# Gate and up projections of a two-layer encoder by seven half-size products for eight

## Chip, cores and metric

One NeuronCore of a Trainium2 chip runs the whole program. The metric is device time in microseconds, the median of several executions; lower is better.

## The reference

The program computes two post-norm layers over 512 tokens of width 1024. Each layer mixes tokens (three groups of attention heads and an output projection), adds the result to the scaled input, normalises, and then applies a SwiGLU feed-forward of width 2816. Weights, inputs and outputs are float32. What the change touches is the first half of the feed-forward:

```python
x = layer_norm(DN_ALPHA * x + mix, ln1_g[l], ln1_b[l])
ff = (jax.nn.silu(x @ ffn_w_gate[l]) * (x @ ffn_w_up[l])) @ ffn_w_down[l]
x = layer_norm(DN_ALPHA * x + ff, ln2_g[l], ln2_b[l])
```

## The kernel before

A float32 operand is split into two float32r parts, a rounded high part (a cast by ACT) and the residual (a subtraction), and a product is three matmuls into one PSUM bank: high by high, high by residual, residual by high (`mm3`, L162). Weights come by the SP queue as raw float32 tiles of 128x1024 (four of them in turn); `wload` (L142) casts them into `whi` on ACT and takes the residual `wlo` on DVE or POOL. The pools `wh` and `wl` hold four tiles of each kind; some loads put both parts into the pool `pqk` instead (ring "q").

The transposed input of the feed-forward, `xT`, lies as high and residual part, each for all 512 tokens. The 22 blocks of 128 hidden columns are done in two parts, 12 and 10. For each block, `gate_up` (L770) runs 8 slices of depth by 3 matmuls of 512 tokens for gate and the same for up, 48 matmuls; `swiglu` (L776) applies SiLU on ACT (L778), multiplies on DVE (L779), and splits the product into the two parts of an `act` tile on ACT and DVE (L781, L782). Blocks 0 and 1 of a layer run by halves of the tokens, 96 matmuls of 256 columns each, so that they can start before the last tokens are normalised. After each part `down` (L800) multiplies its `act` tiles by rows of the down weights, two row blocks per load; the casts go to the rings `DR` in turn.

POOL does norms, residuals of weights and softmax scaling in the attention stage; in the gate/up blocks it has nothing. The program is written as one stream; a scheduler in the tile framework reorders it once per engine, and each engine then runs its own list in order, with semaphore waits. A tile of a pool can be written again when the last reader of the tile that held its place has finished.

The lines that the text names: L156 is the residual of a weight tile (`lo.tensor_tensor` in `wload`), L152 its cast; L214, L215, L217 and L218 are gain and offset of a layer norm on POOL and DVE; L256 is the softmax scaling on POOL; L272 the residual of transposed probabilities on DVE, from PSUM; L290 a sum from PSUM and SBUF on DVE.

Of the kernel before, what the change touches and what calls it, by code (L numbers as in the profile page):

```python
# [10 lines left out]
F32 = mybir.dt.float32  # L11
# [5 lines left out]
P = 128  # L17
# [64 lines left out]
def encoder(ctx: ExitStack, tc, x, w_in, mla_q_norm, mla_kv_norm, w_uq, w_ukv, gqa_q_norm, gqa_k_norm, rel_bias,  # L82
# [5 lines left out]
    def pool(name, bufs, **k):  # L88
        return ctx.enter_context(tc.tile_pool(name=name, bufs=bufs, **k))
# [72 lines left out]
    def mm3(ps, a, b, first, last):  # L162
        ah, al = a
        bh, bl = b
        TE.matmul(ps, ah, bh, start=first, stop=False)  # L165
        TE.matmul(ps, ah, bl, start=False, stop=False)  # L166
        TE.matmul(ps, al, bh, start=False, stop=last)  # L167

    def make_xT():
        return [pxt.tile([P, NT, KD, P], F32R, tag="x", name=n) for n in ("xTh", "xTl")]  # L170

    def put_xT(xT, t):
        for g in range(2):
            pb = bank(ps_pt, "xtr")
            for f in range(4):
                c = (g * 4 + f) * P
                TE.transpose(pb[:, f * P:(f + 1) * P], xt[:, t, c:c + P], ident)
            pb = pb.rearrange("p (f c) -> p f c", f=4)
            h = xT[0][:, t, g * 4:g * 4 + 4, :]
            A.copy(h, pb)  # L180
            V.tensor_tensor(xT[1][:, t, g * 4:g * 4 + 4, :], pb, h.bitcast(F32), op=ALU.subtract)

    def xst(xT, k, t):
        return xT[0][:, t, k, :], xT[1][:, t, k, :]

# [207 lines left out]
    for l in range(DEPTH):  # L393
# [128 lines left out]

        def mla_T(h):
            assert ("q", h // 3) in told
            to_T(lambda t: tq[0][:, t, h, :], 96, mqk[h])
# [46 lines left out]
            V.tensor_tensor(v, v, tm, op=ALU.add)  # L572

        def latent_qv():
            q = pxt.tile([P, NT, 6, 96], F32, tag="x", name="tq")
            tq.append(q)
            wq = [wload(krows(w_uq[l], 0, 2, 288 * c, 288 * c + 288), (P, 2, 288), LO['uq']) for c in range(2)]
            wkv.append(wload(krows(w_ukv[l], 0, 1, 0, 768), (P, 1, 768), LO['kv']))
            yield
            for c in range(2):  # L580
                h, o = wq[c]
                for t in range(NT):
                    pb = bank(ps_mm, "uq")[:, :288]
# [153 lines left out]
        def finish(t):  # L737
            for half in range(2):
                assert ("op", t, half) in told
                cs = slice(half * 512, half * 512 + 512)  # L740
                V.tensor_tensor(xt[:, t, cs], xt[:, t, cs], accs[t][half], op=ALU.add)
            layer_norm(t, gb)
            if not xT2:
                xT2.append(make_xT())
            put_xT(xT2[0], t)

        def out_early():
            out_rest(0, (0, 1))
# [11 lines left out]
        for t in (2, 3):  # L760
            out_rest(t, (0, 1, 2))
            finish(t)
        xT = xT2[0]


        f0 = 0
        for part, nf in enumerate((12, 10)):
            act = []

            def gate_up(w, pss, tsl):  # L770
                for wt, ps in zip(w, pss):
                    for k in range(KD):
                        xm = (xT[0][:, tsl, k, :], xT[1][:, tsl, k, :])
                        mm3(ps[:, tsl.start * P:tsl.stop * P], (wt[0][:, k], wt[1][:, k]), xm, k == 0, k == KD - 1)

            def swiglu(pss):  # L776
                sg = ppl.tile([P, T], F32, tag="l", name="sg")
                A.activation(sg, pss[0], AF.Silu)  # L778
                V.tensor_tensor(sg, sg, pss[1], op=ALU.mult)  # L779
                a = pmix.tile([P, 2, T], F32R, tag="m", name="act")  # L780
                A.copy(a[:, 0], sg)  # L781
                V.tensor_tensor(a[:, 1], sg, a[:, 0].bitcast(F32), op=ALU.subtract)  # L782
                act.append(a)

            fs = list(range(f0, f0 + nf))
            if part == 0:
                first = [(w, (bank(ps_sc, "gate"), bank(ps_pv, "up"))) for w in first]
                for tsl in (slice(0, 2), slice(2, 4)):
                    for w, pss in first:
                        gate_up(w, pss, tsl)  # L790
                for w, pss in first:
                    swiglu(pss)
                fs = fs[2:]
            for f in fs:
                w = load_gu(f, V, RINGS[f % 2])
                pss = (bank(ps_sc, "gate"), bank(ps_pt, "up"))
                gate_up(w, pss, slice(0, 4))
                swiglu(pss)

            def down(acc, toks, half, lo, lead=0):  # L800

                n = nf // 2
                ws = {}
                for i in range(n + lead * (len(toks) - 1)):
                    if i < n:
                        ws[i] = wload(krows(w_down[l], f0 + 2 * i, 2, half * 512, half * 512 + 512), (P, 2, 512), lo, DR[i % 5], "wd")
                    for q, (t, pb) in enumerate(zip(toks, acc)):
                        c = i - lead * q
                        if not 0 <= c < n:
                            continue  # L810
                        ts = slice(t * P, (t + 1) * P)
                        for j in range(2):
# [52 lines left out]
```

## Time and profile before

| quantity | value |
|---|---|
| median of 3 runs | 1281.17 us (1280.31 to 1282.43) |
| the profiled execution | 1282.31 us |
| its span, first to last instruction | 1280.5 us |
| PE busy | 1250.1 us, 98%, 6352 matmuls |
| DVE busy | 687.7 us, 54% |
| ACT busy | 543.6 us, 42% |
| POOL busy | 324.6 us, 25% |
| mean granted clock of PE | 0.994 |

Busy time is the time in which an engine has an instruction in flight. Matmuls overlap in the pipeline, so that a matmul's length (0.39 us for 512 columns) is longer than the distance to the next; distances are read from the timeline. PEld is the loading of the stationary operand, which overlaps PE. In the timelines a row is one instruction, or several of the same kind in a row (x2, x4) with their joint time.

### The profile page before, as it was taken

The page shows a single profiled execution, that of the slowest core. Times are in us where ns is not written, and L with a number is a line of the kernel's source. Part 1 is how long each engine was busy: PE and PEld are TensorE (multiplying, and loading weights), DVE is VectorE, ACT ScalarE, POOL GpSimd, SP SyncE. Part 2 cuts the span into 40 slices and gives each one's busy share as a digit, 9 for nine tenths or more (in the row PEclk, how much of TensorE's full clock was granted, in tenths as well). Part 3 has the DMA queues.
Part 4 walks back from the last instruction along what each step waited for, and adds up shares of the span by engine and source line. Part 5 has one row for each costly group of instructions (what it writes and reads, how often), then busy time and mean ns, then how long its engine had stood idle before and what let it go on. Part 6 is the DMA issues. An engine that isn't in the chain of part 4 may idle for free.

```text
span 1280.5 us, 16743 instructions
## 1 busy us (share of the span) xinstructions
PE 1250.1 (98%) x6352; PEld 1062.5 (83%) x6352; DVE 687.7 (54%) x1138; ACT 543.6 (42%) x955; POOL 324.6 (25%) x344
## 2 busy tenths in 40 slices
PE   8999899999999999999999998999999999999997
PEld 7888788889888888888898897888988888888885
DVE  4377997684333333332664889966843332333346
ACT  4465786544222212222245668855342221222222
POOL 0445475661000000000245456655500000000004
PEclk9999899999999999999999999999999999999999
DMA  5623210324333233332425231114243333333223
GB/s 179 188 67 87 87 34 13 120 69 130 99 99 97 89 96 98 99 99 99 148 78 147 84 103 48 28 30 134 77 115 99 99 99 99 99 99 98 92 96 110
DMA packets 140552, 122.57 MB, mean 96 GB/s; under 512 B 6924, under 2 KB 114572, under 8 KB 140472
## 3 DMA queue, kind: packets, MB, share of 16 engines
q1 hardware_dynamic: 140460, 121.48, 32.0%
q8 instruction: 50, 0.82, 0.3%
q14 instruction: 30, 0.25, 0.1%
q10 hardware_dynamic: 12, 0.02, 0.0%
HBM read 114.65 MB, written 2.12 MB: 91 GB/s over the span
## 4 chain that ended last, share of the span: by engine, by line
PE 80%; DVE 8%; DMA 4%; ACT 3%; POOL 2%; issue 2%; SPq 0%; DVEq 0%; POOLq 0%; ACTq 0%
PE gate L165 6%; PE down L167 6%; PE down L166 6%; PE up L167 6%; PE down L165 6%; PE up L165 6%; PE up L166 6%; PE gate L167 6%; PE gate L166 6%; PE sc L241 4%; PE ptr L264 3%; PE po L283 2%; PE po L282 2%; PE tp L166 1%; PE tp L165 1%
## 5 line engine op out<-in xcount | busy, mean ns | idle before, releaser
L152 ACT CAST whi<-wraw 128x1024 fp32r<-128x1024 f32 (+3 forms) x202 | 205.6, 1020 | 550.6 <-PE gate L166 149.3
L156 DVE TENSOR_TENSOR wlo<-wraw,whi 128x1024 fp32r<-128x1024 f32 (+3 forms) x170 | 208.2, 1226 | 319.7 <-ACT whi L152 315.7
L191 POOL TENSOR_TENSOR rstd<-mv,eps_l 128x1 f32<-128x1 f32 x16 | 5.7, 357 | 680.8 <-DVE mv L200 680.8
L256 POOL TENSOR_TENSOR pl<-pl,srec 128x512 f32<-128x512 f32 x128 | 135.7, 1061 | 153.0 <-DVE srec L255 139.2
L166 PE MATMUL gate<-xTl,whi 128*128 128x512 f32 (+1 forms) x384 | 142.8, 372 | 0.0
L166 PE MATMUL up<-xTl,whi 128*128 128x512 f32 (+1 forms) x384 | 142.7, 372 | 0.0
L167 PE MATMUL gate<-xTh,wlo 128*128 128x512 f32 (+1 forms) x384 | 142.7, 372 | 0.0
L167 PE MATMUL up<-xTh,wlo 128*128 128x512 f32 (+1 forms) x384 | 142.7, 372 | 0.0
L165 PE MATMUL up<-xTh,whi 128*128 128x512 f32 (+1 forms) x384 | 142.6, 372 | 0.0
L165 PE MATMUL gate<-xTh,whi 128*128 128x512 f32 (+1 forms) x384 | 142.4, 371 | 0.0
L167 PE MATMUL down<-whi,act 128*128 128x512 f32 x352 | 136.7, 389 | 0.0
L166 PE MATMUL down<-wlo,act 128*128 128x512 f32 x352 | 136.7, 389 | 0.0
L165 PE MATMUL down<-whi,act 128*128 128x512 f32 x352 | 136.7, 389 | 0.0
L779 DVE TENSOR_TENSOR sg<-sg,up 128x512 f32<-128x512 f32 x44 | 30.3, 688 | 136.1 <-PE up L167 134.8
L156 POOL TENSOR_TENSOR wlo<-wraw,whi 128x512 fp32r<-128x512 f32 (+2 forms) x64 | 79.4, 1265 | 78.7 <-ACT whi L152 78.4
L272 DVE TENSOR_TENSOR PTl<-ptr,PTh 128x512 fp32r<-128x512 f32 x128 | 87.2, 682 | 8.7 <-ACT PTh L271 7.6
L271 ACT CAST PTh<-ptr 128x512 fp32r<-128x512 f32 x128 | 74.9, 586 | 38.9 <-PE ptr L264 38.4
L167 PEld LDWEIGHTS up<-xTh,wlo 128*128 128x128 f32 x384 | 72.4, 189 | 12.6
L165 PEld LDWEIGHTS gate<-xTh,whi 128*128 128x128 f32 x384 | 72.3, 188 | 12.5
L166 PEld LDWEIGHTS up<-xTl,whi 128*128 128x128 f32 x384 | 72.3, 188 | 12.5
L166 PEld LDWEIGHTS gate<-xTl,whi 128*128 128x128 f32 x384 | 72.4, 188 | 12.4
L165 PEld LDWEIGHTS up<-xTh,whi 128*128 128x128 f32 x384 | 72.3, 188 | 12.4
(174 smaller groups left out, 2493.6 us busy)
## 6 DMA issues: line engine op xcount, KB each, us to landing
wraw<-in_ffn_w_down SPq DMA_DIRECT2D x54, 512.0 KB, 3.6
wraw<-in_ffn_w_up SPq DMA_DIRECT2D x44, 512.0 KB, 3.9
wraw<-in_ffn_w_gate SPq DMA_DIRECT2D x44, 512.0 KB, 3.9
wraw<-in_w_in SPq DMA_DIRECT2D x20, 512.0 KB, 4.7
wraw<-in_w_out SPq DMA_DIRECT2D x14, 512.0 KB, 3.7
dt<-tdr SPq DMA_DIRECT2D x12, 448.0 KB, 3.9
wraw<-in_w_in SPq DMA_DIRECT2D x8, 416.0 KB, 3.4
wraw<-in_w_in SPq DMA_DIRECT2D x8, 384.0 KB, 3.9
```

Of the source, the lines that this page charges most:

```text
L152: A.copy(h[:, :n], r[:, :n])
L156: lo.tensor_tensor(o[:, c:c + step], r[:, c:c + step], h[:, c:c + step].bitcast(F32), op=ALU.subtract)
L165: TE.matmul(ps, ah, bh, start=first, stop=False)
L166: TE.matmul(ps, ah, bl, start=False, stop=False)
L167: TE.matmul(ps, al, bh, start=False, stop=last)
L241: TE.matmul(sc, a, b, start=i == 0, stop=i == len(ops) - 1)
L256: G.tensor_tensor(pl, pl, r.to_broadcast([P, T]), op=ALU.mult)
L264: TE.transpose(pb[:, kt * P:(kt + 1) * P], pl[:, kt * P:(kt + 1) * P], ident)
L271: A.copy(ph[:, :, c:c + P], pb)
L272: V.tensor_tensor(plo[:, :, c:c + P], pb, ph[:, :, c:c + P].bitcast(F32), op=ALU.subtract)
L282: TE.matmul(po[:, h0:h0 + 256], self.vst(kt), ph[:, kt], start=kt == 0, stop=False)
L779: V.tensor_tensor(sg, sg, pss[1], op=ALU.mult)
```

## The change

Blocks 3 to 21 of each layer are computed by a scheme of seven products. The stacked matrix of gate and up columns (2 x 128) over two halves of the depth (2 x 512) is multiplied with the input in two halves of depth and two halves of tokens (256). Instead of eight products of 128 columns by 512 depth by 256 tokens there are seven, of which three have sums of weight quarters as one operand (S1, S2, S3) and sums of input quarters as the other (tf1, tf2, tf3), one has the weight sum S4, and one the input sum tf4:

- `load_forms` takes the two raw tiles of a block, forms the four sums `ws` of 128x512 on POOL (S1, S3, S2, S4 in this order) and casts seven operands into four pairs of `whi`/`wlo` tiles: one cast of 1024 columns (gate, "11" and "12"), five of 512 ("22", "S1", "S2", "S3", "S4"), and their residuals on DVE.
- `by_blocks` runs the seven `product`s, 12 matmuls of 256 columns each, into four banks u0 to u3. Three of the banks take a second product on top of the first, after the first has been copied out. Three copies on ACT (e1, e2), four sums on DVE with one operand in PSUM and one sum on POOL give gate (`sg`) and up; SiLU, product and split follow as before.
- The input lies as four tiles `xF` by depth half and token half; their sums tf1 to tf4 are made once per layer (`diff`, `split4`), three of them on DVE, tf3's difference on POOL.
- Blocks 0, 1 and now 2 run with the plain scheme by halves of the tokens. The parts have 11 and 11 blocks. Since `act` tiles take the place of `pqk`, the weights of `down` are cast into `wh` and `wl` alone. `tq` and the transposed input of the attention stage are cut into smaller tiles of the same pool, with the same operations.

```diff
-    pxt = pool("pxt", 2)
+    pxt = pool("pxt", 4)
...
-        for part, nf in enumerate((12, 10)):
+        for part, nf in enumerate((11, 11)):
...
+            def load_forms(f):
...
+                g1, g2, u1, u2 = g[:, :512], g[:, 512:], u[:, :512], u[:, 512:]
+                s1, s2, s3, s4 = (pv_sb.tile([P, 512], F32, tag="v", name="ws") for _ in range(4))
+                G.tensor_tensor(s1, u1, u2, op=ALU.add)
+                G.tensor_tensor(s3, g1, u1, op=ALU.subtract)
+                G.tensor_tensor(s2, s1, g1, op=ALU.subtract)
+                G.tensor_tensor(s4, g2, s2, op=ALU.subtract)
+                out = {}
+                for group in ((("11", "12"), g), (("22", "S1"), (u2, s1)), (("S2", "S3"), (s2, s3)), (("S4",), (s4,))):
+                    names, src = group
+                    h = wh.tile([P, 1024], F32R, tag="w", name="whi")
+                    o = wl.tile([P, 1024], F32R, tag="w", name="wlo")
+                    if not isinstance(src, tuple):
+                        A.copy(h, src)
+                        V.tensor_tensor(o, src, h.bitcast(F32), op=ALU.subtract)
+                    for i, n in enumerate(names):
+                        c = slice(512 * i, 512 * i + 512)
+                        if isinstance(src, tuple):
+                            A.copy(h[:, c], src[i])
+                            V.tensor_tensor(o[:, c], src[i], h[:, c].bitcast(F32), op=ALU.subtract)
+                        out[n] = (h[:, c], o[:, c])
+                return out
+
+            def product(ps, w, x, more=False):
+                for k in range(4):
+                    c = slice(k * P, k * P + P)
+                    mm3(ps, (w[0][:, c], w[1][:, c]), (x[0][:, k], x[1][:, k]), k == 0 and not more, k == 3, more)
+
+            def by_blocks(w):
...
+                product(r0, w["11"], xb["11"])
+                A.copy(e1[:, :H], r0)
+                product(r1, w["12"], xb["21"])
+                V.tensor_tensor(g[:, :H], r1, e1[:, :H], op=ALU.add)
+                product(r3, w["S1"], tf[1])
+                product(r2, w["S3"], tf[3])
+                A.copy(e1[:, H:], r2)
+                V.tensor_tensor(e2[:, H:], r3, e1[:, H:], op=ALU.add)
+                product(r0, w["S2"], tf[2], True)
+                A.copy(e2[:, :H], r0)
+                G.tensor_tensor(u[:, H:], e2[:, :H], e2[:, H:], op=ALU.add)
+                product(r2, w["22"], tf[4], True)
+                V.tensor_tensor(u[:, :H], r2, e2[:, :H], op=ALU.add)
+                product(r3, w["S4"], xb["22"], True)
+                V.tensor_tensor(g[:, H:], r3, e2[:, :H], op=ALU.add)
+                A.activation(g, g, AF.Silu)
+                V.tensor_tensor(u, g, u, op=ALU.mult)
+                put_act(u)
...
             for f in fs:
-                w = load_gu(f, V, RINGS[f % 2])
-                pss = (bank(ps_sc, "gate"), bank(ps_pt, "up"))
-                gate_up(w, pss, slice(0, 4))
-                swiglu(pss)
+                by_blocks(load_forms(f))
...
-                        ws[i] = wload(krows(w_down[l], f0 + 2 * i, 2, half * 512, half * 512 + 512), (P, 2, 512), lo, DR[i % 5], "wd")
+                        nk = min(2, nf - 2 * i)
+                        ws[i] = wload(krows(w_down[l], f0 + 2 * i, nk, half * 512, half * 512 + 512), (P, nk, 512), lo, "w", "wd")
```

The scheduled orders below show one block in the middle of the first part, where all repeat from block to block. In a row stand the line, the operation, the tile written, the tiles read, the shape and the engines waited for; numbers tell tiles apart.

DVE before, in one gate/up block and the start of the next (`wlo` residual of a weight tile, `sg` product of SiLU and up, `act` its residual):

```order
L782 TENSOR_TENSOR act_3807<-sg_3804,act_3807 128x512 [waits Activation_49]
L156 TENSOR_TENSOR wlo_4086<-wraw_4082,whi_4084 128x1024 [waits DMAHW0_49,PE_49,Activation_49]
L779 TENSOR_TENSOR sg_3872<-sg_3872,up_3823 128x512 [waits PE_49,Activation_49]
L156 TENSOR_TENSOR wlo_3956<-wraw_3952,whi_3954 128x1024 [waits DMAHW1_49,Activation_49]
L782 TENSOR_TENSOR act_3875<-sg_3872,act_3875 128x512 [waits Activation_49]
```

A block has two residuals, the product and its split there, all four at 512 or 1024 columns.

DVE in the changed kernel, in one block (L861 and L866 residuals of operand forms, L886, L890, L895 and L897 sums with a PSUM bank, L899 the product, L829 its residual):

```order
L890 TENSOR_TENSOR e2_4136<-u3_4134,e1_4135 128x256 [waits Activation_49]
L866 TENSOR_TENSOR wlo_4253<-wraw_4238,whi_4252 128x512 [waits DMAHW5_49,PE_49,Activation_49]
L866 TENSOR_TENSOR wlo_4253<-ws_4240,whi_4252 128x512 [waits Activation_49]
L895 TENSOR_TENSOR up_4138<-u2_4133,e2_4136 128x256 [waits PE_49,Activation_49]
L866 TENSOR_TENSOR wlo_4259<-ws_4241,whi_4258 128x512 [waits Activation_49]
L866 TENSOR_TENSOR wlo_4259<-ws_4242,whi_4258 128x512 [waits Activation_49]
L897 TENSOR_TENSOR sg_4137<-u3_4134,e2_4136 128x256 [waits PE_49]
L866 TENSOR_TENSOR wlo_4265<-ws_4243,whi_4264 128x512 [waits Activation_49]
L886 TENSOR_TENSOR sg_4274<-u1_4269,e1_4272 128x256 [waits PE_49,Activation_49]
L899 TENSOR_TENSOR up_4138<-sg_4137,up_4138 128x512 [waits Activation_49,Pool_49]
L861 TENSOR_TENSOR wlo_4386<-wraw_4373,whi_4385 128x1024 [waits DMAHW6_49,Activation_49]
L829 TENSOR_TENSOR act_4233<-up_4138,act_4233 128x512 [waits Activation_49]
```

Four instructions per block have become twelve. The residuals of the block ahead (`wlo_4253` to `wlo_4265`) and of the block after it (`wlo_4386`) stand between the sums of the block that is being multiplied.

POOL in the changed kernel, at the same place (L893 the half-size sum of up; `ws` the operand sums of a block two ahead); before, POOL had no instruction in this stretch:

```order
L893 TENSOR_TENSOR up_4001<-e2_3999 128x256 [waits DVE_49,Activation_49]
L850 TENSOR_TENSOR ws_4240<-wraw_4238 128x512 [waits DMAHW5_49,DVE_49]
L851 TENSOR_TENSOR ws_4242<-wraw_4236,wraw_4238 128x512 [waits DMAHW4_49,DVE_49,Pool_49]
L852 TENSOR_TENSOR ws_4241<-ws_4240,wraw_4236 128x512 [waits DVE_49,Pool_49]
L853 TENSOR_TENSOR ws_4243<-wraw_4236,ws_4241 128x512 [waits DVE_49,Pool_49]
L893 TENSOR_TENSOR up_4138<-e2_4136 128x256 [waits DVE_49,Activation_49]
```

Each operand sum waits for DVE, which frees its `ws` tile by the residual of the block before.

PE in the changed kernel, between two blocks (`u0_3994` is the bank of the block that ends, `u0_4131` and `u1_4132` are those of the next, `whi_4111` and `wlo_4112` its first pair of parts):

```order
L165 MATMUL u0_3994<-tf_3351,whi_3984 128x256
L166 MATMUL u0_3994<-tf_3350,wlo_3985 128x256
L164 MATMUL u0_4131<-xF_3164,whi_4111 128x256 [waits Activation_49]
L165 MATMUL u0_4131<-xF_3164,whi_4111 128x256
L164 MATMUL u1_4132<-xF_3166,whi_4111 128x256
L165 MATMUL u1_4132<-xF_3166,whi_4111 128x256
L166 MATMUL u0_4131<-xF_3164,wlo_4112 128x256 [waits DVE_49]
L164 MATMUL u0_4131<-xF_3164,whi_4111 128x256
```

The first four matmuls of the next block, which read only high parts, are put ahead; the fifth waits for the residual on DVE. Behind it on PE stand products 22 and S4 of the block that ends.

## Rows read from the trace of the kernel before

**Rows 1.** The page: busy time, share and instructions of each engine.
```profile
PE 1250.1 (98%) x6352; PEld 1062.5 (83%) x6352; DVE 687.7 (54%) x1138; ACT 543.6 (42%) x955; POOL 324.6 (25%) x344
```

**Rows 2.** The page: shares of the chain that ended last, by engine.
```profile
PE 80%; DVE 8%; DMA 4%; ACT 3%; POOL 2%; issue 2%; SPq 0%; DVEq 0%; POOLq 0%; ACTq 0%
```

**Rows 3.** Window: PE, PEld, DVE, ACT, POOL busy us (count), clock, DMA share, GB/s.
```profile
306.40:415.00 108.60, 108.60 (x487) 90.17 (x486) 39.01 (x43) 32.39 (x42) 0.00 (x0) 1.00 0.35 104
```

**Rows 4.** Timeline of DVE there: start us, us, engine, line, operation, tiles [idle before].
```profile
395.04 0.69 DVE L779 TENSOR_TENSOR sg<-sg,up 128x512 f32<-128x512 f32 x1 [3.38 <-PE up L167]
396.47 1.22 DVE L156 TENSOR_TENSOR wlo<-wraw,whi 128x1024 fp32r<-128x1024 f32 x1 [0.74 <-ACT whi L152]
397.61 0.68 DVE L782 TENSOR_TENSOR act<-sg,act 128x512 fp32r<-128x512 f32 x1
405.92 0.69 DVE L779 TENSOR_TENSOR sg<-sg,up 128x512 f32<-128x512 f32 x1 [3.42 <-PE up L167]
```

**Rows 5.** Timeline of ACT there.
```profile
395.39 1.05 ACT L152 CAST whi<-wraw 128x1024 fp32r<-128x1024 f32 x1 [4.49 <-DMA wraw<-in_ffn_w_down]
396.34 0.62 ACT L781 CAST act<-sg 128x512 fp32r<-128x512 f32 x1
```

**Rows 6.** Timeline of PE there, 14 spacings of 512 columns.
```profile
399.76 0.39 PE L166 MATMUL gate<-xTl,whi 128*128 128x512 f32 x1
...
402.93 0.39 PE L165 MATMUL up<-xTh,whi 128*128 128x512 f32 x1
```

**Rows 7.** Timeline of PE, 19 spacings of 256 columns, first gate/up group.
```profile
283.10 0.28 PE L165 MATMUL gate<-xTh,whi 128*128 128x256 f32 x1
...
285.37 0.28 PE L167 MATMUL up<-xTh,wlo 128*128 128x256 f32 x1
```

**Rows 8.** Timeline of DVE while its queue is full.
```profile
253.85 1.23 DVE L156 TENSOR_TENSOR wlo<-wraw,whi 128x1024 fp32r<-128x1024 f32 x1 [0.44 <-ACT whi L152]
254.99 0.41 DVE L290 TENSOR_TENSOR mf<-po,pvt 64x256 f32<-64x256 f32 x1
255.33 0.67 DVE L251 TENSOR_REDUCE nm<-sc 128x1 f32<-128x512 f32 x1
255.93 0.67 DVE L272 TENSOR_TENSOR PTl<-ptr,PTh 128x512 fp32r<-128x512 f32 x1
```

**Rows 9.** Timeline of POOL, four sums back to back.
```profile
44.23 5.05 POOL L156 TENSOR_TENSOR wlo<-wraw,whi 128x512 fp32r<-128x512 f32 x4 [43.32 <-ACT whi L152]
```

**Rows 10.** Three source lines: engine, operation, count, ns min/median/max, first and last start.
```profile
L272 DVE TENSOR_TENSOR PTl<-ptr,PTh x128: 668/681/694, 65.1 to 894.3; 128x512 fp32r<-128x512 f32 x128
L156 DVE TENSOR_TENSOR wlo<-wraw,whi x170: 741/1225/2115, 6.8 to 1258.7; 128x1024 fp32r<-128x1024 f32 x152, 128x832 fp32r<-128x832 f32 x8, 128x768 fp32r<-128x768 f32 x6, 128x576 fp32r<-128x576 f32 x4
L256 POOL TENSOR_TENSOR pl<-pl,srec x128: 1032/1042/2094, 58.7 to 890.5; 128x512 f32<-128x512 f32 x128
```

**Rows 11.** Timeline of DVE: L217 with nothing on POOL.
```profile
281.54 0.73 DVE L217 SCALAR_TENSOR_TENSOR xtok<-xtok,mv,lngb 128x512 f32<-128x512 f32 x1
```

**Rows 12.** Timeline of DVE and POOL: L217 beside a POOL sum.
```profile
635.42 1.79 DVE L217 SCALAR_TENSOR_TENSOR xtok<-xtok,mv,lngb 128x512 f32<-128x512 f32 x1
635.38 1.29 POOL L214 TENSOR_TENSOR xtok<-xtok,lngb 128x512 f32<-128x512 f32 x1
```

**Rows 13.** Timeline of POOL beside the first instruction of group 8.
```profile
252.88 3.09 POOL L256 TENSOR_TENSOR pl<-pl,srec 128x512 f32<-128x512 f32 x2
```

**Rows 14.** Windows around two idle stretches of PE: busy time, clock.
```profile
120.00:127.00 7.00, 4.70 (x27) 3.81 (x25) 2.25 (x10) 1.44 (x8) 1.89 (x3) 1.00 0.31 85
145.50:147.00 1.50, 1.50 (x7) 1.50 (x7) 1.50 (x5) 0.15 (x1) 0.23 (x1) 0.50 0.63 236
```

**Rows 15.** Timeline of PE: end of the first idle stretch, and after the second.
```profile
125.87 0.66 PE L264 MATMUL ptr<-tab,pl 128*128 128x128 f32 x4 [2.21 <-POOL pl L256]
146.09 0.41 PE L283 MATMUL po<-PTl,dv 128*128 128x256 f32 x1
...
146.94 0.41 PE L283 MATMUL po<-PTl,dv 128*128 128x256 f32 x1
```

More of the change, by code (lines that the diff above doesn't have):

```diff
@@ L160, in krows, with mm3, xT_at, make_xF @@
         return w[k0 * P:(k0 + nk) * P, c0:c1].rearrange("(k p) c -> p k c", p=P)
-    def mm3(ps, a, b, first, last):
+    def mm3(ps, a, b, first, last, more=False):
         ah, al = a
         bh, bl = b
-        TE.matmul(ps, ah, bh, start=first, stop=False)
-        TE.matmul(ps, ah, bl, start=False, stop=False)
-        TE.matmul(ps, al, bh, start=False, stop=last)
+        TE.matmul(ps, ah, bh, start=first, stop=False, skip_group_check=more)
+        TE.matmul(ps, ah, bl, start=False, stop=False, skip_group_check=more)
+        TE.matmul(ps, al, bh, start=False, stop=last, skip_group_check=more)
     def make_xT():
-        return [pxt.tile([P, NT, KD, P], F32R, tag="x", name=n) for n in ("xTh", "xTl")]
-    def put_xT(xT, t):
+        return [[pxt.tile([P, KD // 2, T], F32R, tag="x", name=n) for n in ("xTh", "xTl")] for _ in range(2)]
+    def xT_at(xT, i, g, t):
+        return xT[g][i][:, :, t * P:(t + 1) * P]
+    def make_xF():
+        return [[pxt.tile([P, 2, KD // 2, T // 2], F32R, tag="x", name="xF") for _ in range(2)] for _ in range(2)]
+    def xF_at(xF, i, g, t):
+        return xF[g][t // 2][:, i, :, (t % 2) * P:(t % 2) * P + P]
+    def put_xT(xT, t, at=xT_at):
         for g in range(2):
@@ L574, in latent_qv @@
         def latent_qv():
-            q = pxt.tile([P, NT, 6, 96], F32, tag="x", name="tq")
-            tq.append(q)
+            tq.extend(pxt.tile([P, NT, 3, 96], F32, tag="x", name="tq") for _ in range(2))
             wq = [wload(krows(w_uq[l], 0, 2, 288 * c, 288 * c + 288), (P, 2, 288), LO['uq']) for c in range(2)]
@@ L762, in encoder, with split4, diff @@
             finish(t)
-        xT = xT2[0]
+        xF = xT2[0]
+        def split4(r, h, o):
+            A.copy(h, r)
+            V.tensor_tensor(o, r, h.bitcast(F32), op=ALU.subtract)
+        def diff(e, a, b, b_raw=None):
+            r = pmix.tile([P, KD // 2, T // 2], F32, tag="m", name="tr")
+            ah, al = (a[:, i].bitcast(F32) for i in range(2))
+            if b_raw is not None:
+                e.tensor_tensor(r, ah, b_raw, op=ALU.subtract)
+                e.tensor_tensor(r, r, al, op=ALU.add)
+                return r
+            bh, bl = (b[:, i].bitcast(F32) for i in range(2))
+            e.tensor_tensor(r, ah, bh, op=ALU.subtract)
+            e.tensor_tensor(r, r, al, op=ALU.add)
+            e.tensor_tensor(r, r, bl, op=ALU.subtract)
+            return r
@@ new lines, in two @@
+        def two():
+            return [pmix.tile([P, KD // 2, T // 2], F32R, tag="m", name="tf") for _ in range(2)]
+        (b11, b12), (b21, b22) = xF
+        tf = {}
+        r3 = diff(G, b22, b12)
+        r1 = diff(V, b12, b11)
+        tf[1] = two()
+        split4(r1, *tf[1])
+        r2 = diff(V, b22, None, r1)
+        tf[2] = two()
+        split4(r2, *tf[2])
+        tf[3] = two()
+        split4(r3, *tf[3])
+        r4 = diff(V, b21, None, r2)
+        f4 = pxt.tile([P, 2, KD // 2, T // 2], F32R, tag="x", name="tf4")
@@ L779, in swiglu @@
                 V.tensor_tensor(sg, sg, pss[1], op=ALU.mult)
[L780 to L783, printed above, removed]
+                put_act(sg)
+            def load_forms(f):
+                raw = []
+                for w in (w_gate, w_up):
+                    turn["raw"] += 1
+                    pl, tg = raws["wwdd"[turn["raw"] % 4]]
+                    r = pl.tile([P, 1024], F32, tag=tg, name="wraw")
+                    nc.sync.dma_start(r.rearrange("p (a c) -> p a c", a=KD), krows(w[l], 0, KD, f * P, f * P + P))
+                    raw.append(r)
+                g, u = raw
+                g1, g2, u1, u2 = g[:, :512], g[:, 512:], u[:, :512], u[:, 512:]
[19 more added lines that the diff above has]
+                return out
@@ new lines, in product @@
+            def product(ps, w, x, more=False):
[3 more added lines that the diff above has]
+            def by_blocks(w):
+                H = T // 2
+                r0, r1, r2, r3 = (bank(p, n)[:, :H] for p, n in ((ps_mm, "u0"), (ps_sc, "u1"), (ps_pt, "u2"), (ps_pv, "u3")))
+                e1 = pmf.tile([P, T], F32, tag="m", name="e1")
+                e2 = pg.tile([P, T], F32, tag="g", name="e2")
+                g = ppl.tile([P, T], F32, tag="l", name="sg")
+                u = ppl.tile([P, T], F32, tag="l", name="up")
+                product(r0, w["11"], xb["11"])
[16 more added lines that the diff above has]
+                put_act(u)
@@ L811, in down @@
                         ts = slice(t * P, (t + 1) * P)
-                        for j in range(2):
+                        for j in range(min(2, nf - 2 * c)):
                             a = act[2 * c + j]
```

48 lines of the change are left out of this document (30 added, 18 removed).

## The prediction

> **What bounds the kernel now.** I read the page first, then windows and timelines of the gate/up stretch, then the places where VectorE (DVE) and GpSimd (POOL) work at once. The page gives TensorE (PE) 98% of the span against 54, 42 and 25% for DVE, ScalarE (ACT) and POOL [rows 1], and 80% of the chain that ended last [rows 2]. Between 306.4 and 415 us, ten gate/up blocks, PE is never idle at a granted clock of 1.00; DVE is busy 39 us, ACT 32 us and POOL not at all [rows 3]. The product line L779 returns after 405.92 - 395.04 = 10.88 us: one block of 128 hidden columns [rows 4]. It is 48 matmuls of 512 columns, one every (402.93 - 399.76)/14 = 0.2264 us [rows 6], 10.87 us. So PE alone sets this stretch, and the reader should note the empty POOL column: the change fills it.
>
> **What is removed.** A block by seven products has 7 x 4 x 3 = 84 matmuls of 256 columns. Their spacing stands in the trace, in the first group of gate/up: (285.37 - 283.10)/19 = 0.1195 us [rows 7], so 84 take 10.04 us. Half the columns cost 53% of the time, so the saved eighth shrinks from 1.36 to 10.88 - 10.04 = **0.84 us** per block. Blocks 3 to 21 of both layers, 38 of them, would give 31.9 us. Block 2 joins the two that work by halves of the tokens: 96 x 0.1195 = 11.47 us, 0.59 more, 1.2 us for both layers.
>
> **What is added, by busy time.** Per block DVE now makes five residuals of 512 columns, one of 1024, the product, its residual and four sums of 256 columns with one input in PSUM. Start to start these take 0.60, 1.14, 0.60, 0.60 and 0.34 us (255.33 to 255.93, 253.85 to 254.99, 254.99 to 255.33) [rows 8]: 7 x 0.60 + 1.14 + 4 x 0.34 = 6.7 us. ACT has one cast of 1024 columns at 0.95 (395.39 to 396.34) and ten operations of at most 512 at no more than 0.62 [rows 5], 7.2 us at most. POOL has four sums of 512 columns at 5.05/4 = 1.26 [rows 9] and one of 256, for which I take 0.7: 5.7 us. Each is below 10.04, so by busy time PE would go on setting the pace.
>
> **DVE and POOL at once.** This decides the sum. L217, a DVE instruction with both tensors in SBUF, takes 0.73 us with nothing on POOL [rows 11]. Issued 0.04 us after a POOL sum of 1.29 us had begun, it took 1.79 [rows 12]: 1.06 us longer. The other way round, a DVE residual begun at 253.85 lies under the second of two POOL multiplications that take 3.09 us [rows 8, 13] where each takes 1.04 by its median [rows 10]: about 1.0 us lost. The residual L156, both inputs in SBUF, ranges from its 1.23 us to 2.12, and L256 on POOL from 1.04 to 2.09; L272, whose first input is in PSUM, never leaves 668 to 694 ns in 128 instructions [rows 10]. So a DVE instruction with two SBUF inputs and a POOL instruction exclude each other, and DVE gets through about 1.06 us after POOL began, 0.2 us before POOL's end. Of DVE's twelve instructions per block eight have two SBUF inputs, and all five of POOL's count.
>
> The Trainium skill, "SBUF — State Buffer", section "Who interferes with whom", says that a Vector instruction with two SBUF inputs contends with a GpSimd one that reads SBUF and that the second fully blocks until the first finishes. By that rule a block would cost the sum's whole 1.29 us rather than the 1.06 measured [rows 12], a case of its own below. It speaks against this change.
>
> **Whether it reaches PE.** The orders in the section on the change fix this. A block's operand forms fill all four casting buffers, so the form "22" of block f+1 is cast only after product 22 of block f has been read. From there the chain is, from the start of product 22: eleven spacings and the last matmul, 11 x 0.1195 + 0.28 = 1.59; ACT's cast 0.62 [rows 5]; hand-offs, 0.03 us in 396.44 to 396.47 [rows 4, 5], taken as 0.1 for both; then DVE in its order as far as the 1024-column residual of block f+2, six of 0.60, three of 0.34 and 1.22, in all 5.84; then PE, whose next eight matmuls waited for that residual, 8 x 0.1195 = 0.96, and product 22 of the next block begins. Total 9.1 us, under PE's own 10.04: without POOL 0.9 us is spare and PE never waits.
>
> POOL's four operand sums for block f+2 all fall into this DVE stretch, because each waits until DVE's residual of the block before has freed its 512-column buffer (the DVE waits in the order of POOL). A held-back instruction gets its turn when the other's ends, so the two alternate and each sum delays DVE by up to 1.06 us: 4.2 us. At two of the places DVE has a sum with a PSUM input next, which may run meanwhile (less 2 x 0.34), and the half-size sum may cost up to 0.5, taken as 0.2: **3.7 us**. A block then takes 9.1 + 3.7 = **12.8 us**, 1.92 more than now, and PE idles 2.8 us of it, most in one piece before the first matmul that reads the new residual. The ends: no delay gives 10.04, five full ones 9.1 + 4.2 + 0.5 = 13.8. I take 12.8 because the alternation is what the rows nearest to it show.
>
> The last two blocks of each run have no sums two blocks ahead on POOL, 4 per layer, and go at 10.04.
>
> **The sum,** against the profiled execution's 1282.3 us (span 1280.5; the median of the runs is 1.1 lower):
> - 30 blocks at 12.8 for 10.88: +57.6
> - 8 blocks at 10.04: -6.7
> - block 2 by halves: +1.2
> - the token forms at the head: some 12 DVE instructions of 1.14 and 11 of 0.60, 20 us, and up to 10 of blocking, under the 23 us of PE work in the three first blocks and the 7 us of the next products: 0 to 4 per layer, taken as 1, +2
> - down projection: casts rotate through four buffers instead of six, and the (11, 11) split adds a half-size load per column pass. A pair of row blocks costs PE 24 matmuls of 0.2264, 5.4 us for four tokens, against ACT's 1.05 and DVE's 1.23; in the last pass, with two tokens at a time, 2.7 us against 2.4 with hand-offs. Covered, barely: 0 to 3 per layer, taken as 1, +2. The SP queue issues six more weight loads, none at a wait: DMA is busy 0.35 of the time [rows 3].
>
> Attention, norms, final output: the same instructions, at nothing. Together +56: 1338.4 profiled, **1337 us** as a median. With blocks from 11.8 to 13.3 and the small terms at their ends this case reaches from about 1303 to 1362.
>
> **Rivals.**
> - *The sums find DVE's pauses* (faster). Of 12.8 us DVE would be idle 12.8 - 6.7 - 3.7 = 2.4 us, before the cast of "22", and a POOL sum is wanted only one block later. If the sums drift there, no more than 0.9 us of blocking is left on the chain and PE sets the pace: -31.9 + 1.2 + 2 gives 1253.6, **1252** as a median. Against it: both engines run in program order, and what frees POOL's sums lies behind the cast. Chance 0.12. Break-even is at about 1.75 us of blocking per block.
> - *Half-way.* The sums cost 1 to 2.7 us instead of 3.7: blocks of 10.2 to 11.8, 1258 to 1303. Chance 0.10.
> - *Blocking for the whole sum*: 4 x 1.29 - 0.7 + 0.25 = 4.7, blocks of 13.8, +30 us on the forecast: **1367**. The early start of L217 speaks against it [rows 12]. Chance 0.08. It is what the Trainium skill's rule above gives.
> - *The clock falls in PE's pauses.* The window with a 2.21 us pause kept a clock of 1.00, but after two pauses with one short matmul between them it stood at 0.50, the level of 1.2 GHz [rows 14, 15], and 256 columns took (146.94 - 146.09)/4 = 0.2125 us. Twenty such matmuls after each pause are 20 x 0.093 = 1.9 us in 30 blocks, +56: **1393**. PE's pauses here would be 2.4 us with 0.5 us of work before them. Chance 0.06.
> - That the change does not do what it says I exclude: the order of PE shows the 84 matmuls.
>
> **How the numbers follow.** Forecast 0.64, rivals 0.12, 0.10, 0.08, 0.06. About 0.2%, 2.6 us, is what a measurement here can tell from no change. Faster takes the first rival and a little of the second, 0.13; same 0.02; slower 0.85. The range leaves out the fast rival, the clock and a part of the second: 1275 to 1380.
>
> **What would show it.** Right: POOL busy for about half of the gate/up stretch where it was idle; DVE residuals with a median well above their 0.69 and 1.23 us and maxima near 1.7 and 2.3; product 22 returning every 12 to 13.5 us; PE's idle time released by the DVE residual. The sums with PSUM inputs stay near 0.41. Wrong: blocks of 10.0 us with PE never idle, or residuals at their old durations beside busy POOL, or a granted clock below 1.00 in this stretch.

## The result, and the profile of the changed kernel

The changed kernel takes **1293.95 us** (median of 4 runs, 1291.51 to 1295.16) beside 1280.74 us (4 runs, 1279.96 to 1282.43) for the kernel before: a ratio of 1.0099 with a 95% interval of 1.0081 to 1.0117, slower by 1.0%. The direction and the range were right; the size, 13 us where 56 were forecast, was not. The profiled execution, the shortest of the four, took 1291.51 us, span 1289.7; against the profiled execution of before it is 9.2 us longer, and that difference is the one taken apart here.

The page of the changed kernel, to be read against [rows 1, 2]: busy time and chain by engine, and the costliest lines of two groups (busy us, mean ns of one | idle time before, releaser).

```profile
PE 1232.5 (96%) x7816; PEld 1111.4 (86%) x7816; DVE 973.7 (75%) x1470; ACT 658.2 (51%) x1235; POOL 624.1 (48%) x540
PE 56%; DVE 25%; ACT 6%; POOL 5%; issue 4%; DMA 4%; DVEq 0%; SPq 0%; ACTq 0%; POOLq 0%
L866 DVE TENSOR_TENSOR wlo<-ws,whi 128x512 fp32r<-128x512 f32 x152 | 159.4, 1068 | 3.2
L166 PE MATMUL u<-xF,wlo 128*128 128x256 f32 x456 | 125.4, 290 | 17.8 <-DVE wlo L861 17.8
```

DVE's share of the chain has gone from 8 to 25%, and PE sits idle before one group of matmuls, released by the residual L861. Two windows inside the two runs of blocks of the first layer, columns as in [rows 3]:

```profile
341.00:395.00 54.00, 51.92 (x424) 50.92 (x423) 52.81 (x61) 29.84 (x56) 36.52 (x25) 1.00 0.34 99
475.00:600.00 125.00, 120.33 (x931) 116.08 (x930) 110.18 (x129) 65.56 (x118) 68.29 (x47) 1.00 0.34 100
```

In the first, DVE is busy 52.8 of 54 us: here it sets the pace. In the second it sets it only up to 573 us, where the sums of the last block are done. POOL is busy 68% and 55% of the windows where it was idle; the clock stays at 1.00.

**The balance.** I take each start of a matmul to the next, less the usual spacing for that number of columns, as PE's wait, and add it up by what waited:

| against the kernel before | us |
|---|---|
| PE's work at its usual spacing (1226.5 to 1196.8) | -29.7 |
| waits in 28 blocks, 0.78 each | +21.8 |
| waits in the first two blocks by products of each layer, 2.7 and 0.2 (first at 328.8 and 961.1 us) | +5.8 |
| waits at the head of the gate/up stretch, both layers: transposes 4.1, gate 2.5 | +6.6 |
| transposes at the end of layer 0 (657.8 and 659.9 us) | +2.9 |
| from the last matmul's start to the end (8.90 to 11.66) | +2.75 |
| all else | -1.0 |
| span, 1280.5 to 1289.7 | **+9.2** |

So the saved products are there, 29.7 of the 30.7 us forecast (31.9 less 1.2), and are given back in five places.

**One block.** The timeline of DVE over one period, from one sum L890 to the next, 374.45 - 363.58 = 10.87 us:

```profile
363.58 0.41 DVE L890 TENSOR_TENSOR e<-u,e 128x256 f32<-128x256 f32 x1
363.92 0.68 DVE L866 TENSOR_TENSOR wlo<-wraw,whi 128x512 fp32r<-128x512 f32 x1
364.52 1.22 DVE L866 TENSOR_TENSOR wlo<-ws,whi 128x512 fp32r<-128x512 f32 x1
365.88 0.42 DVE L895 TENSOR_TENSOR up<-u,e 128x256 f32<-128x256 f32 x1
366.40 1.87 DVE L866 TENSOR_TENSOR wlo<-ws,whi 128x512 fp32r<-128x512 f32 x2
368.19 0.41 DVE L897 TENSOR_TENSOR sg<-u,e 128x256 f32<-128x256 f32 x1
368.53 1.45 DVE L866 TENSOR_TENSOR wlo<-ws,whi 128x512 fp32r<-128x512 f32 x1
369.90 0.41 DVE L886 TENSOR_TENSOR sg<-u,e 128x256 f32<-128x256 f32 x1
370.24 1.45 DVE L899 TENSOR_TENSOR up<-sg,up 128x512 f32<-128x512 f32 x1
371.61 2.31 DVE L861 TENSOR_TENSOR wlo<-wraw,whi 128x1024 fp32r<-128x1024 f32 x1
373.85 0.68 DVE L829 TENSOR_TENSOR act<-up,act 128x512 fp32r<-128x512 f32 x1
374.45 0.41 DVE L890 TENSOR_TENSOR e<-u,e 128x256 f32<-128x256 f32 x1
```

POOL in the same period:

```profile
364.14 1.05 POOL L893 TENSOR_TENSOR up<-e 128x256 f32<-128x256 f32 x1 [2.16 <-DVE e L890]
365.81 1.30 POOL L850 TENSOR_TENSOR ws<-wraw 128x512 f32<-128x512 f32 x1 [0.63 <-DVE wlo L866]
367.80 1.63 POOL L851 TENSOR_TENSOR ws<-wraw 128x512 f32<-128x512 f32 x1 [0.68 <-POOL ws L850]
369.39 1.74 POOL L852 TENSOR_TENSOR ws<-ws,wraw 128x512 f32<-128x512 f32 x1
371.21 1.62 POOL L853 TENSOR_TENSOR ws<-wraw,ws 128x512 f32<-128x512 f32 x1
```

Against lengths of 0.68 (512 columns) and 1.22 (1024) with nothing on POOL, five places on DVE are longer: 0.54, 0.58 (the pair, 1.29 when nothing holds it), 0.77, 0.77 and 1.09, in all 3.75 us, next to the 3.7 forecast. The four sums with an input in PSUM stay at 0.41. What is not there is the forecast's pause of 2.4 us: 6.7 us of DVE's own work, the forecast's figure, and 3.75 of lengthening leave 0.42 of the 10.87.

The rows also show when the hold ends. The residual of 368.53 is 0.77 longer, so it gets through at 369.30, and POOL's L851 ends at 367.80 + 1.63 = 369.43; that of 371.61 gets through at 372.70, and L853 ends at 372.83. In all five places it is about 0.13 us before POOL's recorded end. What an instruction on DVE loses is therefore what is left of POOL's when it arrives: these five come 0.4 to 0.8 us after POOL's began.

Why the pause is missing here can be read from ACT and PE. ACT's cast of the form "22" of the next block, then the last matmul of product S2 and the first of product 22 of this block:

```profile
372.94 0.62 ACT L865 CAST whi<-wraw 128x512 fp32r<-128x512 f32 x1 [0.33 <-ACT e L889]
```
```profile
372.69 0.28 PE L166 MATMUL u<-tf,wlo 128*128 128x256 f32 x1
...
373.98 0.39 PE L166 MATMUL u<-xF,wlo 128*128 128x256 f32 x1 [0.52 <-DVE wlo L861]
...
375.03 0.28 PE L164 MATMUL u<-tf,whi 128*128 128x256 f32 x1
```

The cast runs when S2 has been read, 2.1 us before product 22 of this block begins. That fits a form put in the place that came free first (that of S2 and S3) and not in that of the block before with its own name. The second row of PE is its wait: 0.52 us of idle time until L861 is through, and 0.78 per block by starts of matmuls, against the usual 0.12.

**The head.** POOL at the last token tile's norm; then PE waiting for it:

```profile
288.94 1.28 POOL L850 TENSOR_TENSOR ws<-wraw 128x512 f32<-128x512 f32 x1
290.18 0.19 POOL L201 TENSOR_TENSOR rstd<-mv,eps_l 128x1 f32<-128x1 f32 x1
290.32 1.29 POOL L851 TENSOR_TENSOR ws<-wraw 128x512 f32<-128x512 f32 x1
291.57 1.29 POOL L852 TENSOR_TENSOR ws<-ws,wraw 128x512 f32<-128x512 f32 x1
292.82 0.55 POOL L202 TENSOR_TENSOR rstd<-rstd,mhalf 128x1 f32<-128x1 f32 x1
293.33 1.27 POOL L853 TENSOR_TENSOR ws<-wraw,ws 128x512 f32<-128x512 f32 x1
```
```profile
295.43 0.63 PE L187 MATMUL xtr<-tab,xtok 128*128 128x128 f32 x4 [1.54 <-DVE xtok L228]
296.73 0.39 PE L164 MATMUL gate<-xF,whi 128*128 128x256 f32 x1 [0.67 <-ACT xF L190]
```

Of the four sums of block 3 one stands ahead of step L201 of a norm that PE waits for, and two stand between L201 and L202: 2.6 us of L851 and L852 alone.

**The end.** The last two token tiles come out of the down projection (L949 on DVE) at 1277.15 and 1278.51 us, 1.36 apart, where they came 4.08 apart before (1267.96 and 1272.04). Both norms now run almost wholly after PE's last matmul (1278.08 us); before, the first ran beside PE's work on the last tile.

### The profile page after: what moved, and what is told of

The parts are those of the page before. It is cut to its first block, busy times and chain, and to the rows that moved or that the text cites. A ratio compares the mean times of both kernels' runs of the same rounds, so it can differ in the third digit from the quotient of the medians.

```text
span 1289.7 us, 20823 instructions
## 1 busy us (share of the span) xinstructions
PE 1232.5 (96%) x7816; PEld 1111.4 (86%) x7816; DVE 973.7 (75%) x1470; ACT 658.2 (51%) x1235; POOL 624.1 (48%) x540
## 4 chain that ended last, share of the span: by engine, by line
PE 56%; DVE 25%; ACT 6%; POOL 5%; issue 4%; DMA 4%; DVEq 0%; SPq 0%; ACTq 0%; POOLq 0%
PE down L164 6%; PE down L166 6%; PE down L165 6%; DVE wlo L861 5%; DVE wlo L866 5%; PE u L166 4%; PE sc L251 4%; PE u L164 4%; PE u L165 4%; DVE up L899 3%; PE ptr L274 3%; PE tp L164 2%; PE tp L165 2%; PE tp L166 2%; PE po L293 2%
## 5 line engine op out<-in xcount | busy, mean ns | idle before, releaser
L154 DVE TENSOR_TENSOR wlo<-wraw,whi 128x1024 fp32r<-128x1024 f32 (+3 forms) x100 | 122.0, 1226 | 113.1 <-ACT whi L150 113.1
L166 PE MATMUL u<-tf,wlo 128*128 128x256 f32 x608 | 172.1, 283 | 0.0
L165 PE MATMUL u<-tf,whi 128*128 128x256 f32 x608 | 172.1, 283 | 0.0
L164 PE MATMUL u<-tf,whi 128*128 128x256 f32 x608 | 171.8, 283 | 0.0
L866 DVE TENSOR_TENSOR wlo<-ws,whi 128x512 fp32r<-128x512 f32 x152 | 159.4, 1068 | 3.2
L166 PE MATMUL u<-xF,wlo 128*128 128x256 f32 x456 | 125.4, 290 | 17.8 <-DVE wlo L861 17.8
L865 ACT CAST whi<-ws 128x512 fp32r<-128x512 f32 x152 | 90.4, 619 | 99.0 <-PE u L165 78.0
L164 PE MATMUL u<-xF,whi 128*128 128x256 f32 x456 | 127.8, 283 | 1.2 <-ACT whi L860 1.2
L165 PE MATMUL u<-xF,whi 128*128 128x256 f32 x456 | 126.0, 283 | 0.0
L165 PEld LDWEIGHTS u<-tf,whi 128*128 128x128 f32 x608 | 116.8, 192 | 0.2
L166 PEld LDWEIGHTS u<-tf,wlo 128*128 128x128 f32 x608 | 116.8, 192 | 0.0
L164 PEld LDWEIGHTS u<-tf,whi 128*128 128x128 f32 x608 | 116.6, 192 | 0.2
L166 PEld LDWEIGHTS u<-xF,wlo 128*128 128x128 f32 x456 | 84.8, 191 | 24.2 <-DVE wlo L861 24.0
L893 POOL TENSOR_TENSOR up<-e 128x256 f32<-128x256 f32 x38 | 41.7, 1098 | 113.9 <-DVE e L890 63.7
```

What stands on the lines that cost most here:

```text
L154: lo.tensor_tensor(o[:, c:c + step], r[:, c:c + step], h[:, c:c + step].bitcast(F32), op=ALU.subtract)
L164: TE.matmul(ps, ah, bh, start=first, stop=False, skip_group_check=more)
L165: TE.matmul(ps, ah, bl, start=False, stop=False, skip_group_check=more)
L166: TE.matmul(ps, al, bh, start=False, stop=last, skip_group_check=more)
L865: A.copy(h[:, c], src[i])
L866: V.tensor_tensor(o[:, c], src[i], h[:, c].bitcast(F32), op=ALU.subtract)
```

## The experiments

### The four sums on DVE

```diff
-                G.tensor_tensor(s1, u1, u2, op=ALU.add)
-                G.tensor_tensor(s3, g1, u1, op=ALU.subtract)
-                G.tensor_tensor(s2, s1, g1, op=ALU.subtract)
-                G.tensor_tensor(s4, g2, s2, op=ALU.subtract)
+                V.tensor_tensor(s1, u1, u2, op=ALU.add)
+                V.tensor_tensor(s3, g1, u1, op=ALU.subtract)
+                V.tensor_tensor(s2, s1, g1, op=ALU.subtract)
+                V.tensor_tensor(s4, g2, s2, op=ALU.subtract)
```

> The four operand sums of a block move from POOL to DVE. Theory A (DVE and POOL exclude each other, and the 3.7 us that DVE loses to POOL fill it): DVE's own work becomes 6.7 + 4 x 0.60 = 9.1 us per block, with at most 0.5 us lost to POOL's one remaining half-size sum, below PE's 10.04. Blocks take 10.0 to 10.3 us instead of 10.86, about -20 us in 30 blocks, and the total is 1268 to 1277 us. Rival B (DVE's own load and order set the 10.86 us, POOL's share is incidental): 2.4 us more on DVE make blocks of about 13.2 us, +70 us, 1360 or more.

Measured: 1265.29 us (4 runs, 1263.23 to 1266.31) beside 1281.70 (7 runs), ratio 0.9871, 0.9854 to 0.9888: faster than before by 1.3%. That is 3 us under A's range and far from B's. The window of the first blocks:

```profile
341.00:395.00 54.00, 54.00 (x453) 54.00 (x452) 50.23 (x86) 32.35 (x59) 5.14 (x5) 1.00 0.36 108
```

The two residuals, by line (ns min/median/max, first and last start):

```profile
L866 DVE TENSOR_TENSOR wlo<-ws,whi x152: 674/685/1134, 314.6 to 1185.1; 128x512 fp32r<-128x512 f32 x152
L861 DVE TENSOR_TENSOR wlo<-wraw,whi x38: 1207/1218/1226, 308.2 to 1177.2; 128x1024 fp32r<-128x1024 f32 x38
```

The changed kernel has 676/1219/1461 and 1212/2315/2321 there. DVE took over four instructions of 0.68 us per block and its busy time in the window fell, from 52.8 to 50.2 us, while PE went from 51.9 to 54.0 of 54: the sums cost DVE more on POOL (3.75 us of lengthening, 0.54 of it from the half-size sum that stays there) than as its own (4 x 0.60).

### Two sums on DVE, two on POOL

```diff
-                G.tensor_tensor(s1, u1, u2, op=ALU.add)
+                V.tensor_tensor(s1, u1, u2, op=ALU.add)
...
-                G.tensor_tensor(s2, s1, g1, op=ALU.subtract)
+                V.tensor_tensor(s2, s1, g1, op=ALU.subtract)
```

> Two of the four sums (S1 and S2) on DVE, S3 and S4 on GpSimd: half the dose. Theory A (each GpSimd sum costs DVE about 0.75 to 0.85 us per block by exclusion, each DVE sum 0.69 us; DVE is what a block waits for only while its own work and the losses are over 10.05 us): DVE has about 6.7 + 1.4 + 2.2 + 0.4 = 10.7 us if the losses halve with the sums, less if a GpSimd sum finds DVE idle; blocks between 10.1 and 10.6 us, 1266 to 1284 us. Rival L (one GpSimd sum on the chain S1, S3, S2, S4 is enough to keep the block at 10.86 us): 1289 to 1296.

Measured: 1278.04 us (1 run), blocks 10.36 to 10.37 us apart, waits of blocks 12.0 us in sum. DVE: 6.7 + 2 x 0.60 of its own, L866 longer by 0.28 on average over four (963 against 683 ns in the window 363.6 to 407), L899 by 0.78 (1466): 9.8 us, and 0.6 left for hand-offs. Theory A holds with half the dose; rival L falls.

```profile
L866 DVE TENSOR_TENSOR wlo<-ws,whi 128x512 fp32r<-128x512 f32 x16 | 15.1, 963 | 0.0
L899 DVE TENSOR_TENSOR up<-sg,up 128x512 f32<-128x512 f32 x4 | 5.9, 1466 | 0.0
```

### A constant in place of the sums

```diff
-                G.tensor_tensor(s1, u1, u2, op=ALU.add)
+                G.memset(s1, 0.5)
+                G.memset(s1, 0.5)
...
```

> The four sums are left out: POOL instead writes the same four tiles twice each with a constant, at the same places and with the same waits, reading nothing from SBUF. Theory A (exclusion by reads of SBUF): the residuals on DVE are back at 0.68 and 1.23 us and blocks take 10.0 to 10.2 us, total 1268 to 1275. Rival C (DVE waits for POOL's results or for semaphores, whatever POOL does): blocks stay at 10.8 to 10.9 us, total 1290 to 1296.

Measured: 1275.94 us (1 run). The blocks come 10.08 us apart and their waits are gone (0.0 us); POOL meanwhile writes eight tiles per block, 0.53 us each:

```profile
L870 DVE TENSOR_TENSOR wlo<-ws,whi x152: 681/684/693, 323.6 to 1195.1; 128x512 fp32r<-128x512 f32 x152
L865 DVE TENSOR_TENSOR wlo<-wraw,whi x38: 1217/1225/1226, 314.9 to 1186.8; 128x1024 fp32r<-128x1024 f32 x38
```

None of these residuals is held. So POOL's being busy does not hold these instructions; its reading does. That is theory A by the blocks, and C falls. The time is 1 us over A's range and 11 over that of the run with the sums on DVE because the writes, which wait for no weights, crowd the norms at the head: transposes wait 15.4 us and gate matmuls 5.8 (10.4 and 2.3 in the changed kernel).

### One input read in place of two

```diff
-                G.tensor_tensor(s1, u1, u2, op=ALU.add)
+                G.tensor_copy(s1, u1)
...
```

> The four sums are left out: GpSimd copies one operand of each to the sum's tile (one input read from SBUF in place of two), so the blocks multiply other weights. Theory J (GpSimd holds DVE off whenever it reads SBUF at all, one operand or two): DVE's residuals beside a copy stay near the length of the copy, well above 0.69 us, and the loss per block is between a third and all of the 3.7 us; blocks 10.3 to 10.9 us. Theory K (only an instruction with two operands in SBUF holds DVE off): residuals beside copies 0.69 and 1.23 us, blocks 10.05 to 10.15 us as with the constants; then the time is 1264 to 1276, by how much the shorter copies delay the last norm at the head.

Measured: 1270.82 us (1 run), blocks 10.08 us apart. Neither theory has all of it: the time is K's, the mechanism J's.

```profile
L861 DVE TENSOR_TENSOR wlo<-wraw,whi x38: 1210/1627/1632, 312.0 to 1181.6; 128x1024 fp32r<-128x1024 f32 x38
L851 POOL COPY ws<-wraw x38: 608/1013/2150, 292.0 to 1179.1; 128x512 f32<-128x512 f32 x38
```

A copy takes 0.61 us alone and 1.01 by its median, and L861 waits 0.40 us for one: one input on POOL excludes DVE as two do. Being half as long, the copies cost DVE about 0.5 us per block, and PE's 10.08 covers it.

### The places of the forms: their order, then fixed

The first edit lets S2 and S3 take a place ahead of "22" and S1:

```diff
-(("22", "S1"), (u2, s1)), (("S2", "S3"), (s2, s3))
+(("S2", "S3"), (s2, s3)), (("22", "S1"), (u2, s1))
```

> The pairs of forms are allotted in the order S2/S3 before 22/S1, so that the cast of 22 takes the place of the 22 of the block before and waits for its product, as the prediction had assumed. Theory D (this wait was absent in the changed kernel, and is what the forecast of 12.8 us had too much): blocks grow to 11.1 to 12.0 us, total +8 to +35 us. Rival E (DVE is full either way, the wait is covered): blocks stay at 10.8 to 10.9 us.

Measured: 1296.2 us (1 run). Two blocks take 22.0 us (the product L899 returns after 9.48 and 12.53 by turns), 11.0 on average: between D's 11.1 and E's 10.86. Blocks waited 31.2 us in sum, for 27.6. The cast of "22" does stand behind the last matmul of product 22 that reads its high part:

```profile
387.15 0.28 PE L165 MATMUL u<-tf,whi 128*128 128x256 f32 x1
387.52 0.62 ACT L865 CAST whi<-wraw 128x512 fp32r<-128x512 f32 x1 [0.40 <-ACT e L892]
```

With that wait in place DVE has one pause to speak of, 0.69 us, in two blocks. The time lies between the two theories, so the second edit gave each pair of forms a place of its own:

```diff
+            held = [(wh.tile([P, 1024], F32R, tag="w", name="whi"), wl.tile([P, 1024], F32R, tag="w", name="wlo"))
+                    for _ in range(4)]
...
-                for group in ((("11", "12"), g), ...
+                for (h, o), group in zip(held, ((("11", "12"), g), ...
```

> The changed kernel with one thing made as the prediction had assumed it: each of the four pairs of form tiles keeps one place through all blocks of a half layer, so that the form 22 of the next block can be cast only when product 22 of this block has been read. Sums on GpSimd as in the change. Theory M (the prediction's chain was right and only this place was not as assumed): DVE stands idle about 2 us in each block again, blocks of 12 to 12.9 us, u waits of 60 to 90 us in sum, 1320 to 1360 us. Rival N (DVE's work and its losses to GpSimd fill a block of about 10.9 us however the places are given, other residuals or a changed order of the products filling the pause): blocks up to 11.4 us, below 1312 us.

Measured: 1290.63 us (1 run), blocks 10.80 us apart, waits of blocks 20.6 us: rival N. ACT's cast of "22" waits for product 22 here too, whose last matmul starts at 378.18:

```profile
378.43 0.62 ACT L863 CAST whi<-wraw 128x512 fp32r<-128x512 f32 x1 [0.99 <-PE u L165]
```

And DVE still has no pause. Its order has changed with the edit (residuals of other forms stand ahead of that of "22"), and in the timeline from 374.30 to 385.10 one instruction follows the other:

```profile
374.30 1.21 DVE L859 TENSOR_TENSOR wlo<-wraw,whi 128x1024 fp32r<-128x1024 f32 x1
...
376.64 1.78 DVE L864 TENSOR_TENSOR wlo<-ws,whi 128x512 fp32r<-128x512 f32 x1
...
378.67 1.66 DVE L864 TENSOR_TENSOR wlo<-ws,whi 128x512 fp32r<-128x512 f32 x1
...
380.58 0.89 DVE L864 TENSOR_TENSOR wlo<-wraw,whi 128x512 fp32r<-128x512 f32 x1
...
381.74 1.45 DVE L864 TENSOR_TENSOR wlo<-ws,whi 128x512 fp32r<-128x512 f32 x1
...
383.44 1.74 DVE L897 TENSOR_TENSOR up<-sg,up 128x512 f32<-128x512 f32 x1
385.10 1.21 DVE L859 TENSOR_TENSOR wlo<-wraw,whi 128x1024 fp32r<-128x1024 f32 x1
```

Its lengthening is 1.10 + 0.98 + 0.21 + 0.77 + 1.06 = 4.1 us, and 6.7 + 4.1 is the block's 10.8. The block did not grow. Both edits changed DVE's order too, so what the wait would cost in the order of the changed kernel is not shown.

### Block 3's sums alone on DVE

```diff
-            def load_forms(f):
+            def load_forms(f, E=G):
...
-                G.tensor_tensor(s1, u1, u2, op=ALU.add)
+                E.tensor_tensor(s1, u1, u2, op=ALU.add)
...
-                by_blocks(load_forms(f))
+                by_blocks(load_forms(f, V if f == 3 else G))
```

> Only the operand sums of the first block by products (block 3 of each layer) move to DVE. Theory F (those four sums stand on POOL between the steps of the last token tile's norm and delay the transposes): PE's waits before transposes fall by 3 to 5 us in all, blocks stay at 10.86, total -3 to -6 us. Rival G (the norm is late for another reason, or the wait only moves to block 3): total unchanged within 2 us.

Measured: 1292.13 us (1 run), by the whole time inconclusive: its attention stage, which the edit doesn't touch, waited 3 us longer. In the stages that it does touch, gate matmuls wait 0.5 us for 2.3, transposes 8.9 for 10.4, the first blocks 0.6 more: 2.7 us less, just short of theory F's 3; the transposes alone fell by 1.5. In part the wait only moved, as rival G has it: the one at 295.4 us is gone, and the next transposes, at 297.46, wait 1.21 us. Of the head's 6.6 us the order on POOL explains half; a wait of 1.7 us in the second layer (at 921.7) is the same in this run, and the cause of the other half was not tried.

### Sums on DVE and one more casting ring

```diff
-... (P, nk, 512), lo, "w", "wd")
+... (P, nk, 512), lo, "wmwmw"[i % 5] if part else "w", "wd")
```

> The four sums on DVE as before, and in the second half of each layer the cast weights of the down projection go by turns into the weight ring and into the two-place-wide ring of the mixing tiles, so that five pairs of places stand where four did. Theory H (the end and the waiting transposes at the end of layer 0 come from the shortage of casting places, the last weight chunk being cast late): against the run with the sums on DVE alone (1265.3 us) the 2.75 us after the last matmul and the 2.5 us of the transposes at 642.6 and 644.3 go, 1260 us, between 1258 and 1262.5; the last two token tiles end about 4 us apart again. Rival I (the last weight residual is late because VectorE and GpSimd hold each other up, 1.78 us for one, and not because a place is missing): 1264 to 1266.5, time after the last matmul still 11.6 us.

Measured: **1260.58 us** (5 runs, 1259.77 to 1262.05) beside 1281.51 (9 runs), ratio 0.9835, 0.9822 to 0.9849: faster than before by 1.65%, and than the sums on DVE alone by 4.7 us. The last two tiles on DVE:

```profile
1245.68 0.69 DVE L949 SCALAR_TENSOR_TENSOR xtok<-xtok,down 128x512 f32<-128x512 f32 x1 [4.08 <-PE down L166]
...
1249.34 0.68 DVE L949 SCALAR_TENSOR_TENSOR xtok<-xtok,down 128x512 f32<-128x512 f32 x1
```

They stand 3.66 us apart again, the end after the last matmul is 9.72 us for 11.65, and the transposes at the end of layer 0 no longer wait (8.9 to 5.9 us over the kernel). Theory H: the missing places were the cause of nearly all the waiting there and of 1.9 of the 2.75 us at the end.

## Why the prediction was right and where it failed

- **Saved work:** right. 29.7 us less of PE's work.
- **DVE's busy time, exclusion, its price:** right. 6.7 us of own work fits, with 3.75 us of lengthening for 3.7; medians of 1219 and 2315 ns, sums with PSUM inputs at 0.41; without POOL's four sums the blocks go at 10.08, which is PE's own pace. That the price came out so close is partly luck: the four sums cost 3.21 where 4.2 less 0.68 was forecast, the half-size sum 0.54 where 0.2 was. The Trainium skill, "SBUF — State Buffer", section "Who interferes with whom", adds that a GpSimd instruction which only writes does not contend; the run with the constant agrees (684 ns median, 693 at most). Its rule of full blocking agrees with the trace to about 0.13 us: in all five places DVE is held until that long before POOL's recorded end. They lost less than a whole sum of 1.28 us, 0.54 to 1.09, because DVE's instruction came after the sum had begun; the 1.29 us that the prediction drew from the rule would be the loss of one that arrives as the sum begins.
- **The step that failed** is the chain: "the form "22" of block f+1 is cast only after product 22 of block f has been read", and with it the 9.1 us that the 3.7 were added to. 2.4 of the 9.1 were a pause of DVE. The cast came 2.1 us ahead of product 22, and where two edits made it wait, other residuals filled the pause, nearly or wholly, and the block took 11.0 and 10.80. What sets the block is the larger of two sums: PE's 10.08, or DVE's own work, its lengthening and the hand-offs (0 to 0.6 us here, taken as what is left over). That gives 10.87 for the change (6.7 + 3.75 + 0.42), 10.37 with two sums moved and 10.80 with fixed places; with all four moved it is PE's turn. The term "30 blocks at 12.8" was +57.6 and came out as 28 blocks at 10.87, -0.3: the whole miss of 43 us and more. That 10.87 is also the old 10.88 is chance.
- **Last blocks:** forecast -6.7 for eight at 10.04. The other ten went at 10.08, -8.0, but four of them, the first two of each layer, waited as well, +5.8, which the sum had not.
- **Head:** forecast +2, measured +6.6. DVE's load was costed and POOL's order was not: two sums of block 3 stand between two steps of a norm. Moving that block's sums to DVE gave back 3.3 us of these waits; the cause of the rest stays open. The prediction named POOL's queue only inside the blocks.
- **Down projection:** forecast +2 for casts in four places. PE inside it waits no longer than before, yet +2.9 at the end of layer 0 and +2.75 at the very end, 5.7 in all, belong to it: a late last weight chunk moves the first of two tiles onto the second.
- **Rivals.** The time lies in the range of "half-way" (1258 to 1303), by another road: it had cheaper blocking on the same chain, and blocking came at the forecast's price on a shorter one. "The sums find DVE's pauses" supposed a pause that is not there. "Blocking for the whole sum" had too high a price: 3.75 us of lengthening per block, where it needed 4.7. The clock stayed at 1.00 in both windows, but PE's pauses were 0.52 us and not 2.4, so this rival's condition never arose and these runs do not test it.

## What to carry to other kernels

Before an instruction goes to an idle engine, price it on the engine that it will hold up: here a sum costs DVE 0.60 us as its own work, or 0.58 to 1.09 in lengthening from POOL. When a loop is scheduled with operands ready one round ahead, take the larger of the engines' sums, with losses included, before a chain of waits; a pause in a hand-drawn chain is only real if the engine has nothing else in its queue that is ready. Look at both ends of a stretch too: 18 of the 40 us given back lie at the head, at the entry and at the ends of the layers.

## What the runs showed that was not expected

A copy of 512 columns on POOL (0.61 us) excludes DVE's two-input instructions like a sum of 1.28 us, so the number of inputs on POOL sets how long, not whether. And the hold ends at a fixed point: of the two-input instructions on DVE that the changed kernel's POOL lengthened by more than 0.1 us, all 157, over both layers, got through 0.13 to 0.14 us before POOL's recorded end. Two engines that exclude each other lose together: POOL's sums went from 1.28 to a median of 1.63 us (L851) while DVE's residuals went from 0.68 to 1.22, so moving the four sums to the faster engine shortened even DVE's own busy time (52.8 to 50.2 us in the window of 54).
